# A two-block transformer kernel: the pool of operand slots moved to the upper end of the memory, above the weights' buffers

## The chip, the cores and the metric

The kernel runs on one core of a Trainium2 chip. The metric is the device time of one execution in microseconds (us). The core has TensorE (PE; its weight loads are listed as PEld), VectorE (DVE), ScalarE (ACT), GpSimd (POOL) and SyncE (SP), which here only issues DMAs. Operands lie in the on-chip memory SBUF, 128 partitions side by side; an address below is the byte at which a tile begins in each partition. Matmul results go to PSUM, a separate memory that the change does not touch.

## The reference

One sequence of 256 tokens with 1024 features passes through two blocks. The first has two layers: a gated linear recurrence (HGRN2) and a chunked band attention, each with a SwiGLU feed-forward network, all modulated by a vector c. The second mixes four kinds of attention (MoBA, NSA, differential, sliding window) and ends with a convolutional feed-forward network. All is float32. Nearly all of the arithmetic is in products of activations with weight matrices:

```
q, z_f, v, g = split(u @ w_in)                  # layer 0: HGRN2
h = h + g1 * mix;   u = modulate(rms_norm(h))
h = h + g2 * ((silu(gate) * up) @ w_out)        # gate, up = split(u @ w_in)
k, v = split(u @ w_kv);  q = u @ w_q            # layer 1: band attention
mix = concat(moba, nsa, diff, swa) @ w_out      # second block
x = x + rms_norm(conv_ffn(rms_norm(x)))
```

## The kernel before

Activations are kept transposed, features on the partitions and 256 tokens along each row. To reach float32 precision with fast matmuls, each operand is split into two float32r parts, hi and lo, and each product is three matmuls (`mm3`, L257 to L260): hi with hi, hi with lo, lo with hi. In `lin_A` (L262), `out_proj` (L302) and the feed-forward network's `down_T` the weights are loaded into the array and an activation of 256 columns is streamed; in `lin_B` (L280), `lin_Bt` and `down_B` an activation is loaded and the weights are streamed, in 512, 256 or 268 columns.

Weights arrive in units of up to 1088 float32 values per partition. `emit_dma` (L181) loads a unit into one of seven `w_raw` buffers through SP's queue, `emit_conv` (L188) makes `w_hi` on ACT (L193) and `w_lo` on DVE (L195), four buffers each. `pump` (L201) issues loads and conversions ahead of use, and `run` (L224) goes through a list of steps whose order is written out by hand. The instructions' order is therefore fixed when the program is built.

Memory is divided into pools (L144 to L147). `cst` holds constants. `big` holds eight operand slots `s0` to `s7` of 8,192 bytes, taken with `slot(i)` (L152): the residual stream `h` (s0), the hi and lo parts of the normed activations (s1 and s2, later also s3 to s7), the hidden activations (s5, s7), queries, keys and values. The inputs x are loaded into s5 and s6 (L389, L394, L396). `wts` holds the weights' buffers, `wk` small work tiles (`sq`, `nt`, `sig`, `rstd`, ...). Pools of the phases (`open_phase`, L161) hold tiles such as `att`, `lk`, `lq`, `pt` and the partial sums `ga`; they are opened and closed one after the other. A pool goes on top of the last one at the lower end of the memory, or, with `side="right"`, below the last one at the upper end. Before, only `wts` lies at the upper end. Line L350 takes 288 bytes without use (`gap`) among the constants, after which the slots begin at 30,720, a multiple of 2,048.

Of the kernel before, what the change touches and what calls it, by code (L numbers as in the profile page):

```python
# [131 lines left out]
def kernel(ctx: ExitStack, tc: tile.TileContext, x, c, mod_w, mod_b, norm_mix, norm_ffn,  # L132
# [9 lines left out]
    PE, DV, SC, GP, SY = nc.tensor, nc.vector, nc.scalar, nc.gpsimd, nc.sync  # L142

    cst = ctx.enter_context(tc.tile_pool(name="cst", bufs=1))  # L144
    big = ctx.enter_context(tc.tile_pool(name="big", bufs=1))
    wts = ctx.enter_context(tc.tile_pool(name="wts", bufs=1, side="right"))
    wk = ctx.enter_context(tc.tile_pool(name="wk", bufs=2))  # L147
    phase = {}
# [1749 lines left out]
```

## Time and profile before

| | |
|---|---|
| median of 3 runs | 1136.26 us (1135.9 to 1138.14) |
| profiled execution | 1137.38 us, of which the span from the first to the last instruction is 1135.6 us |
| mean granted TensorE clock | 0.996 |
| PE busy / weight loads | 97% / 89% |
| DVE, ACT, POOL busy | 67%, 50%, 12% |
| read from HBM | 239.33 MB, 212 GB/s over the span |

Busy time of PE counts overlapping matmuls; how far two starts are apart, in the timeline, tells the pace. In the rows, `pb_b<-s,w_hi` means that the matmul writes PSUM tile pb_b and reads a slot and w_hi; which of both is streamed is told by its place: the streamed operand stands first in these names where it is an activation (`s,w_hi`: the slot is streamed), and `w_hi,s` means that the weights are streamed and the slot is loaded. Buffer numbers are left out, so `s` is any of the eight slots.

### The profile page before, as it was taken

Reading aid. Unit: us, or ns where it says so; the run is one execution under the profiler, and the core shown is the slowest. Engines: PE = TensorE matmul, PEld = TensorE weight load, DVE = VectorE, ACT = ScalarE, POOL = GpSimd, SP = SyncE. Lnnn points to the kernel's source line nnn. Section 1 sums busy time; section 2 is a strip of 40 time slices with the busy share of each in tenths; the row PEclk is TensorE's granted clock in tenths of the full one; section 3 lists DMA queues with packets and bytes.
Section 4 is the critical chain, followed back from the end, with each engine's and each line's share of the span. In section 5 each row is a group of like instructions: output and inputs, shape, how many; then the busy total and the mean of one; then the engine's idle time right before and its main releaser. Section 6 shows DMA issues by size and latency. Waiting matters only on the chain.

```text
span 1135.6 us, 23604 instructions
## 1 busy us (share of the span) xinstructions
PE 1098.3 (97%) x9689; PEld 1014.6 (89%) x9689; DVE 763.1 (67%) x1237; ACT 572.9 (50%) x913; POOL 141.7 (12%) x201
## 2 busy tenths in 40 slices
PE   6899999999999999999999999999989999999997
PEld 4887888999999978788999999988879999999997
DVE  3577885777677598776555455677766766666676
ACT  2456464543444565655444344646655454454454
POOL 4044410000000001240000000024322110010010
PEclk9999999999999999999999999999998999999999
DMA  9976687898998597865765565873342655655651
GB/s 275 297 256 233 220 272 236 289 311 273 303 303 274 199 294 232 272 225 191 225 213 186 186 203 148 171 196 122 112 148 89 216 179 186 196 175 186 197 175 56
DMA packets 176124, 241.92 MB, mean 213 GB/s; under 512 B 18712, under 2 KB 142160, under 8 KB 176016
## 3 DMA queue, kind: packets, MB, share of 16 engines
q1 hardware_dynamic: 174928, 239.54, 66.8%
q8 instruction: 76, 1.25, 0.4%
q0 software_dynamic: 912, 0.81, 0.4%
q14 instruction: 32, 0.26, 0.1%
q10 hardware_dynamic: 176, 0.07, 0.0%
HBM read 239.33 MB, written 1.05 MB: 212 GB/s over the span
## 4 chain that ended last, share of the span: by engine, by line
PE 84%; DVE 5%; ACT 4%; DMA 3%; POOL 2%; issue 1%; SPq 0%; DVEq 0%; ACTq 0%; POOLq 0%
PE pb_b L258 15%; PE pb_b L260 15%; PE pb_b L259 14%; PE pb_acc L258 11%; PE pb_acc L260 10%; PE pb_acc L259 10%; DMA w_raw<-in_a_w_in_dram 2%; ACT w_hi L193 2%; DVE w_lo L195 2%; PE pb_b L463 1%; POOL dp L860 1%; PE pb_gv L524 1%; PE pb_b L1222 1%; DVE nt L573 1%; DMA w_raw<-in_mod_w_dram 1%
## 5 line engine op out<-in xcount | busy, mean ns | idle before, releaser
L195 DVE TENSOR_TENSOR w_lo<-w_raw,w_hi 128x1024 fp32r<-128x1024 f32 (+1 forms) x335 | 408.4, 1243 | 165.4 <-ACT w_hi L193 164.8
L258 PE MATMUL pb_b<-s,w_hi 128*128 128x256 f32 x1488 | 420.3, 282 | 5.3 <-ACT s L1756 2.9
L260 PE MATMUL pb_b<-s,w_lo 128*128 128x256 f32 x1488 | 417.4, 281 | 1.6 <-DVE w_lo L195 1.5
L259 PE MATMUL pb_b<-s,w_hi 128*128 128x256 f32 x1488 | 417.8, 281 | 0.3
L193 ACT CAST w_hi<-w_raw 128x1024 fp32r<-128x1024 f32 (+1 forms) x336 | 342.2, 1044 | 88.7 <-DMA w_raw<-in_a_w_in_dram 23.5
L258 PEld LDWEIGHTS pb_b<-s,w_hi 128*128 128x128 f32 x1488 | 281.0, 189 | 12.8 <-issue 4.0
L260 PEld LDWEIGHTS pb_b<-s,w_lo 128*128 128x128 f32 x1488 | 280.9, 189 | 2.5 <-DVE w_lo L195 2.4
L259 PEld LDWEIGHTS pb_b<-s,w_hi 128*128 128x128 f32 x1488 | 281.0, 189 | 1.9 <-DVE s L585 0.7
L258 PE MATMUL pb_acc<-s,w_hi 128*128 128x256 f32 x720 | 205.2, 285 | 1.8 <-ACT w_hi L193 1.7
L260 PE MATMUL pb_acc<-s,w_lo 128*128 128x256 f32 x720 | 201.5, 280 | 2.6 <-DVE w_lo L195 2.6
L259 PE MATMUL pb_acc<-s,w_hi 128*128 128x256 f32 x720 | 201.0, 279 | 0.1
L258 PEld LDWEIGHTS pb_acc<-s,w_hi 128*128 128x128 f32 x720 | 135.3, 188 | 9.2 <-issue 5.0
L260 PEld LDWEIGHTS pb_acc<-s,w_lo 128*128 128x128 f32 x720 | 135.3, 188 | 3.4 <-DVE w_lo L195 3.4
L259 PEld LDWEIGHTS pb_acc<-s,w_hi 128*128 128x128 f32 x720 | 135.4, 188 | 0.5 <-DVE s L585 0.3
L1215 POOL TENSOR_SCALAR att<-att,sm 128x128 f32<-128x128 f32 (+1 forms) x72 | 46.0, 657 | 617.4 <-DVE sm L1208 338.5
L1069 ACT CAST s<-sig 128x512 fp32r<-128x512 f32 x38 | 23.6, 621 | 117.6 <-DVE sig L1079 117.6
L258 PE MATMUL pb_acc<-w_hi,s 128*128 128x512 f32 x192 | 77.5, 404 | 1.4 <-ACT s L579 1.0
L259 PE MATMUL pb_acc<-w_lo,s 128*128 128x512 f32 x192 | 76.0, 396 | 0.8 <-DVE w_lo L195 0.8
L260 PE MATMUL pb_acc<-w_hi,s 128*128 128x512 f32 x192 | 76.1, 396 | 0.0
L1782 ACT ACTIVATE sig<-att,vb_t,vc_t 128x256 f32<-128x256 f32 x32 | 17.5, 594 | 75.4 <-DVE att L1777 75.4
L1792 POOL TENSOR_TENSOR sig<-sig,rstd 128x512 f32<-128x512 f32 x16 | 22.7, 1422 | 238.6 <-ACT sig L1790 238.6
L1075 ACT ACTIVATE sig<-pb_b 128x512 f32<-128x512 f32 x22 | 13.2, 598 | 75.1 <-PE pb_b L260 75.1
(367 smaller groups left out, 1166.6 us busy)
## 6 DMA issues: line engine op xcount, KB each, us to landing
w_raw<-in_mod_w_dram SPq DMA_DIRECT2D x96, 512.0 KB, 5.2
w_raw<-in_ffn_w_in_dram SPq DMA_DIRECT2D x88, 512.0 KB, 5.3
w_raw<-in_ffn_w_out_dram SPq DMA_DIRECT2D x44, 512.0 KB, 4.8
w_raw<-in_a_w_in_dram SPq DMA_DIRECT2D x32, 512.0 KB, 6.1
w_raw<-in_ffn_w_gate_dram SPq DMA_DIRECT2D x32, 512.0 KB, 3.7
w_raw<-in_ffn_w_up_dram SPq DMA_DIRECT2D x32, 512.0 KB, 5.4
w_raw<-in_ffn_w_down_dram SPq DMA_DIRECT2D x32, 512.0 KB, 3.5
w_raw<-in_kv_mod_w_dram SPq DMA_DIRECT2D x16, 512.0 KB, 5.6
```

What stands on the lines that cost most here:

```text
L193: SC.copy(hi, raw)
L195: DV.tensor_sub(lo, raw, hi.bitcast(F32))
L258: PE.matmul(o, lhsT=whi, rhs=xhi, start=start, stop=False, skip_group_check=True)
L259: PE.matmul(o, lhsT=whi, rhs=xlo, start=False, stop=False, skip_group_check=True)
L260: PE.matmul(o, lhsT=wlo, rhs=xhi, start=False, stop=stop, skip_group_check=True)
L463: PE.matmul(st[:, 0:256], lhsT=mean_d, rhs=sq[:, 256 * m:256 * m + 256], start=j == 0 and m == 0, stop=j == n - 1 and m == 1)
L524: PE.matmul(g[32 * j:32 * j + 32, 0:256], lhsT=by, rhs=r, start=start, stop=stop, tile_position=(0, 32 * j))
L1069: SC.copy(hi, hid)
L1075: SC.activation(sg, g, AF.Silu)
L1215: GP.tensor_scalar(t[:, i, cs], t[:, i, cs], r[:, 2 * b + i:2 * b + i + 1], 1.0, op0=OP.mult, op1=OP.mult)
L1782: SC.activation(zm, am, AF.Identity, bias=vcol("conv_b")[:, f:f + 1], scale=vc_t[:, 64 + f:65 + f])
L1792: GP.tensor_mul(zp, zp, rs_pair())
```

## The change

The pool `big` is given `side="right"`. As it is opened before `wts`, it takes the upper end, and the weights' buffers come directly below it. The work tiles and the phases' pools move down into the room that the slots leave.

```diff
     cst = ctx.enter_context(tc.tile_pool(name="cst", bufs=1))
-    big = ctx.enter_context(tc.tile_pool(name="big", bufs=1))
+    big = ctx.enter_context(tc.tile_pool(name="big", bufs=1, side="right"))
     wts = ctx.enter_context(tc.tile_pool(name="wts", bufs=1, side="right"))
     wk = ctx.enter_context(tc.tile_pool(name="wk", bufs=2))
```

On all five engines the instructions, their order and the semaphores that they wait for are the same in both programs. What differs are the addresses in the built programs:

| tiles | begin before | begin after | moved by | address past a multiple of 64, before and after |
|---|---|---|---|---|
| constants (`early`, `crep`, `late`, ...) | 16,512 to 25,440 | the same | 0 | unchanged |
| slots s5, s6, s0, s3, s4, s7, s1, s2 | 30,720 and on, each 8,192 | 163,808 and on, each 8,192 | +133,088 | 0, then 32 |
| `sq` (3 buffers) | 96,256 and on | 30,720 and on | -65,536 | 0, then 0 |
| other `wk` tiles and the phases' tiles | up to 163,998 | up to 98,462 | -65,536 | unchanged; `att`, `lk`, `lq`, `pt`: 32 |
| `w_raw` (7), `w_hi` (4), `w_lo` (4) | 164,064 to 229,344 | 98,528 to 163,808 | -65,536 | 32, then 32 |

## Rows read from the trace of the kernel before

**Rows 1.** The page: span, and busy time by engine.
```profile
span 1135.6 us, 23604 instructions
PE 1098.3 (97%) x9689; PEld 1014.6 (89%) x9689; DVE 763.1 (67%) x1237; ACT 572.9 (50%) x913; POOL 141.7 (12%) x201
```

**Rows 2.** The page: chain that ended last, by engine and by line.
```profile
PE 84%; DVE 5%; ACT 4%; DMA 3%; POOL 2%; issue 1%; SPq 0%; DVEq 0%; ACTq 0%; POOLq 0%
PE pb_b L258 15%; PE pb_b L260 15%; PE pb_b L259 14%; PE pb_acc L258 11%; PE pb_acc L260 10%; PE pb_acc L259 10%; DMA w_raw<-in_a_w_in_dram 2%; ACT w_hi L193 2%; DVE w_lo L195 2%; PE pb_b L463 1%; POOL dp L860 1%; PE pb_gv L524 1%; PE pb_b L1222 1%; DVE nt L573 1%; DMA w_raw<-in_mod_w_dram 1%
```

**Rows 3.** Groups by line and shape, TensorE: count, busy us, mean ns, idle before.
```profile
L259 PE MATMUL pb_b<-s,w_hi 128*128 128x256 f32 x1488 | 417.8, 281 | 0.3
L259 PEld LDWEIGHTS pb_b<-s,w_hi 128*128 128x128 f32 x1488 | 281.0, 189 | 1.9 <-DVE s L585 0.7 <-DVE s L1758 0.2
L259 PE MATMUL pb_acc<-s,w_hi 128*128 128x256 f32 x720 | 201.0, 279 | 0.1
L259 PE MATMUL pb_acc<-w_lo,s 128*128 128x512 f32 x192 | 76.0, 396 | 0.8 <-DVE w_lo L195 0.8
L259 PEld LDWEIGHTS pb_acc<-w_lo,s 128*128 128x128 f32 x192 | 36.1, 188 | 8.4 <-DVE w_lo L195 1.1
L259 PE MATMUL pb_b<-w_lo,s 128*128 128x256 f32 x32 | 9.0, 281 | 0.0
```

**Rows 4.** Timeline of TensorE, slots streamed: start us, us, engine, line, operation.
```profile
239.75 0.28 PE L260 MATMUL pb_b<-s,w_lo 128*128 128x256 f32 x1
...
242.11 0.28 PE L259 MATMUL pb_acc<-s,w_hi 128*128 128x256 f32 x1
...
289.73 0.28 PE L258 MATMUL pb_b<-s,w_hi 128*128 128x256 f32 x1
...
291.72 0.28 PE L260 MATMUL pb_b<-s,w_lo 128*128 128x256 f32 x1
```

**Rows 5.** Timeline of TensorE, weights streamed, in 512 and in 256 columns.
```profile
483.80 0.39 PE L259 MATMUL pb_acc<-w_lo,s 128*128 128x512 f32 x1
...
486.81 0.40 PE L260 MATMUL pb_acc<-w_hi,s 128*128 128x512 f32 x1
...
807.88 0.28 PE L260 MATMUL pb_b<-w_hi,s 128*128 128x256 f32 x1
...
810.36 0.28 PE L260 MATMUL pb_b<-w_hi,s 128*128 128x256 f32 x1
```

**Rows 6.** Timeline of TensorE, line L463, `sq` or `att` streamed.
```profile
715.91 1.02 PE L463 MATMUL pb_b<-sq,early 128*128 128x256 f32 x4
716.77 1.03 PE L463 MATMUL pb_b<-att,early 128*128 128x256 f32 x4
717.63 1.03 PE L463 MATMUL pb_b<-sq,early 128*128 128x256 f32 x4
```

**Rows 7.** Groups by line and shape, ACT and DVE (last row: ns min/median/max).
```profile
L1198 ACT ACTIVATE att<-att,mx 128x256 f32<-128x256 f32 x40 | 19.8, 496 | 0.0
L518 DVE SCALAR_TENSOR_TENSOR lk<-w_raw,ca,lk 128x512 f32<-128x512 f32 x28 | 20.9, 746 | 0.0
L1317 ACT ACTIVATE s<-s,cols 128x256 fp32r<-128x256 f32 x8 | 3.6, 496 | 2.2 <-DVE s L1314 2.2
L1820 DVE SCALAR_TENSOR_TENSOR ot<-ot,ms,s x4: 743/748/751, 1128.4 to 1131.9; 128x512 f32<-128x512 f32 x4
```

**Rows 8.** Groups by line and shape on POOL, and who waited for it.
```profile
L877 POOL TENSOR_TENSOR s<-s,dp 128x256 f32<-128x256 f32 x20 | 17.7, 898 | 17.1 <-PE pb_b L900 9.6 <-PE pb_b L919 7.4
L1755 POOL TENSOR_TENSOR s<-s,nt 128x256 f32<-128x256 f32 x8 | 6.7, 875 | 17.3 <-DVE nt L1753 17.3
L877 POOL TENSOR_TENSOR s<-s,s 128x256 f32<-128x256 f32 x4 | 4.5, 1140 | 3.6 <-ACT a L908 3.6
PE pb_b L900 <- POOL s L877: 1.3, 1, 1.3
```

**Rows 9.** DMA issues: count, KB each, median us to landing.
```profile
w_raw<-in_mod_w_dram SPq DMA_DIRECT2D x96, 512.0 KB, 5.2
s<-in_x_dram SPq DMA_DIRECT2D x2, 512.0 KB, 4.1
```

## The prediction

> **What bounds the kernel now.** I read the page from the top: span and busy shares, then the chain of waits, then the groups by line and shape, then the timeline of single matmuls. TensorE is busy 97% of the span [rows 1], and 84% of the chain that ended last is TensorE; the three matmul lines L258 to L260 alone hold 15 + 14 + 15 + 11 + 10 + 10 = 75% of it, or 852 us of 1135.6 [rows 2]. The reader should see that nothing else comes near: DVE has 5%, ACT 4%, DMA 3% and POOL 2% of the chain.
>
> So the question is what one matmul costs and whether that depends on where its operands lie. The groups give the counts: 1488 matmuls on each of the three lines into pb_b and 720 into pb_acc stream a slot (`s`) against weights, 3 x (1488 + 720) = 6624 in all, with 128x256 operands; 192 per line stream the weights in 512 columns, and 32 per line in 256 [rows 3]. The busy time of one (281 ns) overlaps with its neighbours, so the pace has to be read from start to start: 289.73 to 291.72 us holds 17 steps, 0.117 us each; 239.75 to 242.11 holds 20 steps, 0.118 us each [rows 4]. 6624 x 0.117 us = 775 us is the part of the span that streams slots.
>
> **The change part by part.** It adds no instruction and removes none; each engine issues the same operations in the same order behind the same waits in both programs. Every effect must come from addresses. There are two moves.
>
> First, everything but the slots and the constants goes down by 65,536 bytes. That is the same shift for the weights' buffers, the work tiles and the tiles of the phases, and 65,536 is a multiple of every power of two up to itself, so their alignment and their distances to each other stay. I cost this at nothing. What it changes is their distance to the slots, which I take with the second move.
>
> Second, the slots go up by 133,088 bytes, which is 65 x 2,048 less 32. Before, each slot begins at a multiple of 2,048; after, each begins 32 bytes past a multiple of 64, as the weights' buffers do in both versions. So kernel before already runs both kinds of operand, and its rows can be set side by side.
>
> - *TensorE, streaming operand.* A slot streamed in 256 columns has a busy time of 281 ns; the weights streamed in 256 columns, which begin 32 bytes past a multiple of 64, have 281 ns too [rows 3]. The cleanest pair is line L463, where the same constant is loaded and the streamed tile is once `sq` (at a multiple of 2,048) and once `att` (32 past a multiple of 64): four `sq` take from 715.91 to 716.77, four `att` from 716.77 to 717.63, 0.86 us each [rows 6]. These are full fp32 matmuls at about half the pace, so they could hide a stall that float32r matmuls would show. The paces of the float32r matmuls bound it: 512 columns of weights take (486.81 - 483.80) / 13 = 0.2315 us, or 0.1158 per 256, and 256 columns of weights take (810.36 - 807.88) / 21 = 0.1181 [rows 5]. Against 0.117 that is -1.2 ns and +1.1 ns for each of 6624 matmuls: -7.9 to +7.3 us. I take 0, because the two ends have opposite signs for the same kind of address, and because slots at unchanged addresses run at 0.117 in one stretch and 0.118 in another [rows 4], so a nanosecond comes and goes without any move.
> - *TensorE, loaded operand.* Loading weights takes 189 ns, loading a slot 188 ns [rows 3]. 0.
> - *ACT and DVE.* The same operation costs the same at both kinds of address: on ACT 496 ns on `att` and 496 ns on slots (128x256), on DVE 746 ns on `lk` and `w_raw` and 748 ns on `ot` with a slot (128x512) [rows 7]. 0, and TensorE covers both engines in most of the span.
> - *POOL.* No row has a two-input POOL operation on misplaced operands alone. The 20 products of line L877 average 898 ns and four others of the same line 1140 ns [rows 8]; if all 20 went to the dearer row it would be 20 x 0.242 = 4.8 us, if they went down to the 875 ns of L1755, -0.5 us. TensorE waited only 1.3 us for L877 in this execution [rows 8], so little of either end reaches the span. I take 0.
> - *Loads into slots.* Only the two loads of x land in slots (median 4.1 us each); loads of the same 512 KB into the misplaced `w_raw` land in 5.2 us, with more queued ahead of them [rows 9]. If x took that, it would be up to 1.1 us late at the very start; below nothing there is no reason to go, since 4.1 is already the shorter. I take 0. The Trainium skill (DMA: Bandwidth & Descriptors, How a descriptor splits into AXI transactions) speaks against the change here: a descriptor that does not begin at a multiple of 256 B starts its first transaction at the boundary below and pays for bytes that it does not use. By it a 4 KB row of x would need 8 more beats on 128, about 6%; as an estimate from that and the two landings that is 0.25 us on each load, and the sum would be 1136.8 instead of 1136.3. No run here shows it yet.
>
> Sum: 0 + 0. The profiled execution took 1137.38 us, 1.8 us of it outside its span of 1135.6 [rows 1]; it lies 1.1 us above the median of the three timed runs, 1136.26, so the forecast on the median's scale is 1136.3 us. The fixed work in it is the same, whatever the layout.
>
> **The rivals.**
>
> *Slower: the stream from a misplaced slot stalls.* Place: the 6624 matmuls that stream a slot. For it: the 256-column stream of weights paces 0.1181 us against 0.117 [rows 4, 5], the only row with a float32r matmul, the same width and the other kind of address. Against it: the 512-column stream, misplaced alike, is the cheapest per column; L463 shows no difference; the slots themselves reach 0.118 at times. Price: 6624 x 1.1 ns = 7.3 us if all of it is on the path. Nearly all matmuls of the three lines pace 775 + 576 x 0.2315 + 96 x 0.118 = 920 us, and the chain holds 852 of them, 93%: 6.8 us, or 1143.1 us. It decides from 2.3 us / (6624 x 0.93) = 0.37 ns a matmul upward, about a third of the difference that this row suggests, so a partial effect gives 1139 to 1143.
>
> *Faster: the placement next to the weights, or the new alignment, gives slots the pace of the 512-column rows.* For it: 0.1158 per 256 columns [rows 5]. Against it: that gain goes as well with the half as many instructions per column, and the 256-column stream of weights doesn't have it. Price: 6624 x 1.2 ns x 0.93 = 7.4 us, or 1128.9.
>
> *Neighbours get in each other's way.* Slots now lie directly above the buffers that DMA, ACT and DVE fill. If reads and writes of close addresses collided, a matmul that streams the weights' own buffers would already show it, and its 512-column pace is the best there is [rows 5]. If it cost the difference of the two slot paces, 1 ns, it would give 6624 x 1 ns x 0.93 = 6.2 us, 1142.4.
>
> *It does not do what it says.* The slots could have stayed where they were; the addresses of the built program exclude it. A change of waits through reused memory is excluded too, since slots share no memory with other tiles in either version.
>
> **How the numbers follow.** No effect: 0.68, with its own range of 1134.0 to 1138.6, 2.3 us to either side (the three runs of before lie between 1135.9 and 1138.14). The stalled stream, full or in part: 0.18; neighbours: 0.06. The fast pace, full or in part: 0.08. A measurement of this kernel can tell about 0.2%, 2.3 us, from no change, and that gives faster 0.08, same 0.68, slower 0.24. The range goes from 1133.6 to 1143.2: it takes in the whole of no effect and the slower cases to their price, and leaves out most of the faster case and what lies beyond the slower ones.
>
> **What would show it.** Right: start to start of L258 to L260 on slots at 0.117 to 0.118 us in the same stretches, weight loads at 188 ns, TensorE's waits as before, x landing within 0.3 us of before. Wrong: a pace on slots of 0.118 to 0.119 or more in stretches that had 0.117 (stalled stream), above all if 512-column matmuls keep 0.2315; or longer ACT, DVE and POOL operations on slots alone, which I have put at nothing.

## The result, and the profile after

The changed kernel is slower: 1151.32 us against 1136.55 us, ratio 1.0123 (95% interval 1.0099 to 1.0146). The forecast was 1136.3 us with a range from 1133.6 to 1143.2. The profiled execution took 1151.56 us.

The first lines of the page, to be read beside [rows 1] and [rows 2], and the groups of TensorE that answer to [rows 3]:

```profile
span 1149.8 us, 23604 instructions
PE 1113.6 (97%) x9689; PEld 1032.9 (90%) x9689; DVE 763.6 (66%) x1237; ACT 572.1 (50%) x913; POOL 140.0 (12%) x201
PE 85%; DVE 5%; ACT 4%; DMA 3%; issue 2%; POOL 1%; SPq 0%; DVEq 0%; ACTq 0%; POOLq 0%
```

```profile
L259 PE MATMUL pb_b<-s,w_hi 128*128 128x256 f32 x1488 | 422.9, 284 | 0.3
...
L259 PE MATMUL pb_acc<-s,w_hi 128*128 128x256 f32 x720 | 204.2, 284 | 0.0
...
L259 PE MATMUL pb_acc<-w_lo,s 128*128 128x512 f32 x192 | 75.1, 391 | 0.8 <-DVE w_lo L195 0.8
...
L259 PE MATMUL pb_b<-w_lo,s 128*128 128x256 f32 x32 | 9.0, 282 | 0.0
```

```profile
L259 PEld LDWEIGHTS pb_b<-s,w_hi 128*128 128x128 f32 x1488 | 285.8, 192 | 1.8 <-DVE s L585 0.7 <-DVE s L1758 0.3
...
L259 PEld LDWEIGHTS pb_acc<-w_lo,s 128*128 128x128 f32 x192 | 36.1, 188 | 7.6 <-DVE w_lo L195 1.1
```

The span grew by 14.2 us, TensorE's busy time by 15.3 us, DVE's by 0.5 us, ACT's and POOL's not at all; the shares of these three in the chain did not grow. So the loss is TensorE's. A matmul that streams a slot went from 281 (279 into pb_acc) to 284 ns, its weight load from 189 to 192 ns. One that streams the weights in 512 columns went the other way, from 396 to 391 ns, and its load, now of a slot at the other kind of address, stayed at 188.

Busy times overlap, so the pace is read from start to start. The first two rows are of the kernel before, the next four of the kernel after: 60 steps in the same part of the program (L258 to L260, no wait in them), and then 21 steps in 512 columns.

```profile
684.07 0.28 PE L258 MATMUL pb_b<-s,w_hi 128*128 128x256 f32 x1
...
691.07 0.28 PE L258 MATMUL pb_acc<-s,w_hi 128*128 128x256 f32 x1
```

```profile
690.21 0.28 PE L258 MATMUL pb_b<-s,w_hi 128*128 128x256 f32 x1
...
697.40 0.28 PE L258 MATMUL pb_acc<-s,w_hi 128*128 128x256 f32 x1
```

```profile
491.30 0.39 PE L260 MATMUL pb_acc<-w_hi,s 128*128 128x512 f32 x1
...
496.07 0.40 PE L260 MATMUL pb_acc<-w_hi,s 128*128 128x512 f32 x1
```

7.00 us / 60 = 116.7 ns before, 7.19 / 60 = 119.8 ns after; three matmuls (one `mm3`) take 350 ns and then 360. In 512 columns it is 4.77 / 21 = 227.1 ns, where [rows 5] gave 231.5.

The same can be taken over a whole trace: from every start of L258 to the next start of L258, where L258, L259 and L260 follow without a wait (some 2020 such triples stream a slot, some 150 stream weights in 512 columns). All paces below are these means. Slots: 117.0 ns before, 119.9 after. 512 columns: 234.1 before, 229.5 after. In 512 columns some 15 triples take 770 to 820 ns where the others take 700 or 680, and how many of these are counted moves the mean by about 1 ns. The sum that follows: 6624 x 2.9 = 19.2 us lost, 576 x 4.6 = 2.6 us gained, and of the 16.6 us the 93% that the prediction put on the path are 15.4; measured 14.2 on the spans and 14.8 on the medians.

What the prediction also put at nothing stayed there. Line L463 takes 0.86 us for four `sq` as in [rows 6], ACT and DVE cost what they cost in [rows 7], POOL what it cost in [rows 8]:

```profile
724.40 1.02 PE L463 MATMUL pb_b<-sq,early 128*128 128x256 f32 x4
725.26 1.03 PE L463 MATMUL pb_b<-att,early 128*128 128x256 f32 x4
```

```profile
L1198 ACT ACTIVATE att<-att,mx 128x256 f32<-128x256 f32 x40 | 19.8, 496 | 0.0
...
L877 POOL TENSOR_TENSOR s<-s,dp 128x256 f32<-128x256 f32 x20 | 17.5, 891 | 17.0 <-PE pb_b L900 9.5 <-PE pb_b L919 7.5
...
L1317 ACT ACTIVATE s<-s,cols 128x256 fp32r<-128x256 f32 x8 | 3.6, 495 | 2.4 <-DVE s L1314 2.4
```

```profile
s<-in_x_dram SPq DMA_DIRECT2D x2, 512.0 KB, 4.7
```

The loads of x landed after 4.7 us instead of 4.1 [rows 9]. The new address need not be the reason: with the slots where the kernel before has them, a later run (slots 0, weights 0) showed 4.9, and with slots 32 bytes lower another (slots 32, weights 32) showed 4.2. The spread between runs hides the 0.25 us that the prediction estimated from the Trainium skill (DMA: Bandwidth & Descriptors, How a descriptor splits into AXI transactions); no run here shows it.

### The profile page after: what moved, and what is told of

Same layout as the page of the kernel before. It is cut to its first block, busy times and chain, and to the rows that moved or that the text cites. A ratio compares the mean times of both kernels' runs of the same rounds, so it can differ in the third digit from the quotient of the medians.

```text
span 1149.8 us, 23604 instructions
## 1 busy us (share of the span) xinstructions
PE 1113.6 (97%) x9689; PEld 1032.9 (90%) x9689; DVE 763.6 (66%) x1237; ACT 572.1 (50%) x913; POOL 140.0 (12%) x201
## 4 chain that ended last, share of the span: by engine, by line
PE 85%; DVE 5%; ACT 4%; DMA 3%; issue 2%; POOL 1%; SPq 0%; DVEq 0%; ACTq 0%; POOLq 0%
PE pb_b L258 15%; PE pb_b L260 15%; PE pb_b L259 14%; PE pb_acc L258 11%; PE pb_acc L260 10%; PE pb_acc L259 10%; DVE w_lo L195 2%; DMA w_raw<-in_a_w_in_dram 1%; ACT w_hi L193 1%; PE pb_b L463 1%; PE pb_b L1222 1%; DMA w_raw<-in_kv_w_dram 1%; PE pb_gv L524 1%; DMA w_raw<-in_mod_w_dram 1%; POOL dp L860 1%
## 5 line engine op out<-in xcount | busy, mean ns | idle before, releaser
L258 PE MATMUL pb_b<-s,w_hi 128*128 128x256 f32 x1488 | 424.8, 285 | 5.1 <-ACT s L1756 2.9
L260 PE MATMUL pb_b<-s,w_lo 128*128 128x256 f32 x1488 | 421.9, 284 | 1.5 <-DVE w_lo L195 1.4
L259 PE MATMUL pb_b<-s,w_hi 128*128 128x256 f32 x1488 | 422.9, 284 | 0.3
L258 PEld LDWEIGHTS pb_b<-s,w_hi 128*128 128x128 f32 x1488 | 285.7, 192 | 12.5 <-issue 4.4
L260 PEld LDWEIGHTS pb_b<-s,w_lo 128*128 128x128 f32 x1488 | 285.9, 192 | 2.4 <-DVE w_lo L195 2.3
L259 PEld LDWEIGHTS pb_b<-s,w_hi 128*128 128x128 f32 x1488 | 285.8, 192 | 1.8 <-DVE s L585 0.7
L258 PE MATMUL pb_acc<-s,w_hi 128*128 128x256 f32 x720 | 208.3, 289 | 1.8 <-ACT w_hi L193 1.8
L260 PE MATMUL pb_acc<-s,w_lo 128*128 128x256 f32 x720 | 204.5, 284 | 1.5 <-DVE w_lo L195 1.5
L259 PE MATMUL pb_acc<-s,w_hi 128*128 128x256 f32 x720 | 204.2, 284 | 0.0
L258 PEld LDWEIGHTS pb_acc<-s,w_hi 128*128 128x128 f32 x720 | 138.4, 192 | 9.1 <-issue 4.8
L260 PEld LDWEIGHTS pb_acc<-s,w_lo 128*128 128x128 f32 x720 | 138.6, 192 | 2.1 <-DVE w_lo L195 2.1
L259 PEld LDWEIGHTS pb_acc<-s,w_hi 128*128 128x128 f32 x720 | 138.5, 192 | 0.2
L258 PE MATMUL pb_acc<-w_hi,s 128*128 128x512 f32 x192 | 76.7, 400 | 1.5 <-ACT s L579 1.0
L259 PE MATMUL pb_acc<-w_lo,s 128*128 128x512 f32 x192 | 75.1, 391 | 0.8 <-DVE w_lo L195 0.8
L260 PE MATMUL pb_acc<-w_hi,s 128*128 128x512 f32 x192 | 75.1, 391 | 0.0
```

The costliest lines, as they stand in the source:

```text
L258: PE.matmul(o, lhsT=whi, rhs=xhi, start=start, stop=False, skip_group_check=True)
L259: PE.matmul(o, lhsT=whi, rhs=xlo, start=False, stop=False, skip_group_check=True)
L260: PE.matmul(o, lhsT=wlo, rhs=xhi, start=False, stop=stop, skip_group_check=True)
```

## The experiments

All kernels below issue the same instructions in the same order; only addresses differ. "Slots 32" means that the slots begin 32 bytes past a multiple of 64, "weights 32" the same of `w_hi` and `w_lo`. Ratios are to the kernel before, with their 95% intervals.

### First four: is it the place, or 32 bytes?

Three theories. A: the distance between slots and weights counts, taken modulo 64 (equal: 360 ns per three; 32 apart: 350). B: the slots' own start counts. C: the place of the pools counts (the upper end, or lying beside the weights' buffers).

The changed layout, with the slots 32 bytes lower and so on a multiple of 64 again:

```diff
 # on the changed kernel
-        lo = wts.tile([P, UNIT], F32R, name="w_lo", ...)[:, :n]
+        lo = wts.tile([P, UNIT], F32R, name="w_lo", ...)[:, :n]; state["pad"] = state.get("pad") or wts.tile([P, 8], F32, name="pad_w", bufs=1)
-            ubox[tag] = (hi, lo)
+            ubox[tag] = (hi, lo); state["pad_s"] = state.get("pad_s") or big.tile([P, 8], F32, name="pad_s", bufs=1)
```

> The changed kernel's layout (slots above the weights' buffers), with 32 bytes of padding behind the slots and behind the weights' buffers: slots begin at multiples of 64 again, the weights' buffers stay 32 past one. Theory A (what counts is where the slot begins relative to the weights, in the address bits below 64: 32 apart 0.117 us, equal 0.120 us a streamed 256-column matmul): 1136 us, pace 0.117. Theory B (what counts is the slot's own start: at a multiple of 64 0.117, past one 0.120): 1136 us as well. Theory C (the place: upper end, next to the weights' buffers): stays at 1151 us, pace 0.120.

Measured: 1136.63 us, ratio 1.0003 (0.9989 to 1.0017), slots at 116.9 ns. Sixty steps of it:

```profile
684.02 0.28 PE L258 MATMUL pb_b<-s,w_hi 128*128 128x256 f32 x1
...
691.02 0.28 PE L258 MATMUL pb_acc<-s,w_hi 128*128 128x256 f32 x1
```

The whole loss is gone with 32 bytes, at the upper end and beside the weights. C is out.

The layout of before, the slots alone 32 bytes lower:

```diff
-    wk = ctx.enter_context(tc.tile_pool(name="wk", bufs=2))
+    wk = ctx.enter_context(tc.tile_pool(name="wk", bufs=2)); wk.tile([P, 8], F32, name="pad_wk", bufs=1)
-    cst.tile([P, 72], F32, name="gap")
+    cst.tile([P, 64], F32, name="gap")
```

> The layout of before, with the slots alone 32 bytes lower (32 past a multiple of 64, as the weights' buffers); work tiles and weights unmoved. Theories A and B: 1151 us, pace 0.120 on slots, and 0.227 for 512 columns as in the changed kernel. Theory C (place): 1136 us, pace 0.117.

Measured: 1154.44 us, ratio 1.0158 (1.0132 to 1.0183), slots at 119.9 ns, 512 columns at 229.1. The loss is made without moving a pool:

```profile
690.31 0.28 PE L258 MATMUL pb_b<-s,w_hi 128*128 128x256 f32 x1
...
697.50 0.28 PE L258 MATMUL pb_acc<-s,w_hi 128*128 128x256 f32 x1
```

Then the weights' buffers 32 bytes lower, alone (slots 0, weights 0), and together with the slots (slots 32, weights 0); the edits are `pad_w` above, and `pad_w` with the smaller gap.

> The layout of before, with the weights' buffers alone 32 bytes lower, so that slots and weights both begin at multiples of 64. Theory A (relative): as the changed kernel, 1151 us, pace 0.120 on slots. Theory B (the slot's own start): pace 0.117 and 1136 us. Theory C: 1136 us.

> The layout of before, with slots 32 past a multiple of 64 and weights' buffers at multiples of 64: the offsets of before, exchanged. Theory A (relative): pace 0.117 and 1136 us. Theory B (the slot's own start): 0.120 and 1151 us. Theory C: 1136 us.

Measured: 1137.56 us, ratio 1.0004 (0.9989 to 1.0020), and 1137.01 us, 0.9994 (0.9981 to 1.0007). The first contradicts A (equal starts modulo 64, and no loss), the second contradicts B (slots 32, and no loss).

### Next four: a pair of misplaced operands?

What was left was theory D: a matmul pays when both its operands are 32 past a multiple of 64. One edit tests its parts, because a buffer of 1088 values has room to write the parts further in; here only `w_lo` (32 bytes further, on a multiple of 64), in the kernel with slots 32 and weights 32:

```diff
-        lo = wts.tile([P, UNIT], F32R, name="w_lo", tag="w_lo", bufs=WT_BUFS)[:, :n]
+        lo = wts.tile([P, UNIT], F32R, name="w_lo", tag="w_lo", bufs=WT_BUFS)[:, 8:8 + n]
```

> Slots begin 32 bytes past a multiple of 64 as in the run that alone had its slots lowered (1154.4 us), w_hi too, but w_lo begins on a multiple of 64. Of every three matmuls two load w_hi and one loads w_lo, so one of three now has no pair of misplaced operands. Theory D (each matmul pays for its own pair: +3 ns only where its streamed and its loaded operand both begin past a multiple of 64): two thirds of the loss stay, three matmuls take 2 x 120 + 117 = 357 ns, about 1148.5 us. Theory E (the stream of matmuls falls into one common rhythm, which any break of the pattern undoes): three matmuls take 350 to 353 ns as before, about 1137 us. Rival F (one misplaced pair in the three is enough for the slow rhythm): 360 ns, about 1154 us.

> The mirror image: slots 32 past a multiple of 64, w_hi on a multiple, w_lo 32 past it. One matmul of three has both operands misplaced. Theory D (each matmul pays for its own pair): one third of the loss stays, 117 + 117 + 120 = 354 ns, about 1142.5 us. Theory E (common rhythm, undone by any break): 350 to 353 ns, about 1137 us. Rival F (one pair is enough): 360 ns, about 1154 us.

Measured: `w_lo` moved, 1146.21 us, ratio 1.0063 (1.0043 to 1.0084), 355 ns per three; `w_hi` moved instead, 1142.53 us, 1.0036 (1.0022 to 1.0050), 353.3 ns per three. The loss comes in parts, more with two bad loads in the three than with one; E (a common rhythm, undone by any break: 1137 us for both) and F (one pair is enough: 1154 us) lie outside both intervals. D comes nearest without hitting: it forecast 357 and 354 ns, 1148.5 and 1142.5 us, the first above its interval.

Then `w_hi` and `w_lo` 16 bytes further (`[:, 4:4 + n]`), with slots 32 and with slots 0:

> Slots 32 past a multiple of 64, w_hi and w_lo 48 past one instead of 32 (w_raw stays). Theory D as 'any start past a multiple of 64 counts': both operands are misplaced, 120 ns per 256 columns, about 1154 us. Theory G, that the two starts must stand at the same place within 64 bytes on top of being misplaced: 117 ns, about 1137 us. If a start on a multiple of 32 is what matters and 48 is worse than 32, more than 120 ns and over 1156 us.

> Slots on a multiple of 64 as in the kernel before, w_hi and w_lo 48 past one instead of 32. Theories D and G both: only one operand is misplaced, 117 ns per 256 columns, about 1136.5 us. If the distance to the next multiple of 64 set a price by itself, another pace; a rhythm at 113.3 ns throughout, as parts of the run with both operands on multiples of 64 showed it, would give about 1136.5 - 6624 x 3.7 ns x 0.93 = 1114 us.

Measured: 1144.46 us, ratio 1.0058 (1.0041 to 1.0075), 355 ns per three; and 1148.95 us, 1.0090 (1.0067 to 1.0113), 352 ns in some stretches and 360 in others. Neither D (1154 and 1136.5 us) nor G (1137 and 1136.5 us) forecasts them. The second is a loss with slots on a multiple of 64.

### D put to use, and its fall

By D the changed kernel could be mended: loaded weights on a multiple of 64, streamed ones (512 columns, which had become faster) left as they were. The same offsets in the layout of before as a control.

```diff
 # on the changed kernel; Unit keeps off; unit_A and unit_row take it, 8 where nothing is given
-        hi = wts.tile([P, UNIT], F32R, name="w_hi", tag="w_hi", bufs=WT_BUFS)[:, :n]
+        hi = wts.tile([P, UNIT], F32R, name="w_hi", tag="w_hi", bufs=WT_BUFS)[:, u.off:u.off + n]
 # (and w_lo the same way)
-        ... [unit_A(w, 256 * i, c0, 2, 512)] ...
+        ... [unit_A(w, 256 * i, c0, 2, 512, 0)] ...
-        ... unit_row(w_out, 256 * (rounds - 1) + P * i) ...
+        ... unit_row(w_out, 256 * (rounds - 1) + P * i, 8 * (down.__name__ != "down_B")) ...
```

> The changed kernel's layout (slots at the upper end, 32 bytes past a multiple of 64) with one thing added: w_hi and w_lo are written 8 values (32 bytes) into their buffers, so that they begin on a multiple of 64, except the units whose weights are streamed in 512 columns (lin_B and down_B, 576 matmuls), which stay 32 past it like the slots that they meet. Theory D (a price for each matmul whose streamed and loaded operand are both 32 past a multiple of 64, +3 ns on 256 columns, and a gain on 512): the 256-column matmuls run at 350 ns per three as in the run with slots 32 and weights 0, the 512-column ones at 229.5 ns instead of 234.1, so 576 x 4.6 ns x 0.93 = 2.5 us below before: about 1134 us, ratio 0.998. If the gain on 512 columns belonged to the upper end or to something else: 1136.5 us. If the pool's place has a part in the loss: over 1140 us.

> The same offsets in the layout of the kernel before: slots at the lower end, 32 past a multiple of 64, weights' buffers on a multiple of 64, and only the weights that are streamed in 512 columns written 32 bytes further in. Theory D: as the run beside it, about 1134 us, ratio 0.998, with 350 ns per three 256-column matmuls and 229.5 ns per 512-column one. Rival: the 512-column pace hangs on w_raw or on the place of the pools, then 1136.5 us and 234 ns.

Measured: the mended changed kernel 1145.54 us, ratio 1.0086 (1.0067 to 1.0104), slots at 118.4 ns; the control 1136.66 us, 1.0003 (0.9986 to 1.0019), slots at 117.0 ns, 512 columns at 229.3 as forecast. (The 2.5 us that this should bring are not shown: 0.998 lies just outside the interval, although the slots' pace is that of before; why is open.) Two kernels that are alike to D differ by 9 us. The first came out where the rival "the pool's place has a part in the loss" had it; the run with slots 64 lower, below, decides on that. Rows of the first, two stretches of sixty steps:

```profile
321.19 0.28 PE L258 MATMUL pb_b<-s,w_hi 128*128 128x256 f32 x1
...
328.39 0.28 PE L258 MATMUL pb_b<-s,w_hi 128*128 128x256 f32 x1
...
684.09 0.28 PE L258 MATMUL pb_b<-s,w_hi 128*128 128x256 f32 x1
...
691.18 0.28 PE L258 MATMUL pb_b<-s,w_hi 128*128 128x256 f32 x1
```

7.20 / 60 = 120.0 and 7.09 / 60 = 118.2 ns: 360 and 355 per three, never 350.

What does differ is the distance, if it is not cut at 64 bytes. Where a slot is streamed it is the loaded operand's start less the streamed one's, that is `w_hi`'s start less a slot's start, modulo 256: 224 before, 0 in the changed kernel, 224 in the two harmless runs with one pool shifted (slots 0 and weights 32 at the upper end; slots 32 and weights 0 at the lower), 192 with slots 0 and weights 0, 32 in the mended kernel. Slots are 8,192 bytes apart and cut at 1,024, buffers 4,352 (17 x 256) and cut at 512, so one number serves for all matmuls of a kernel that stream a slot against weights. This is theory H: the distance alone counts, modulo 256. It is theory A with a longer period, and it was made from these ten runs, so it needed runs that could refute it.

### One number, moved in steps

The slots alone go lower by 64, 96, 128, 160 and 192 bytes in the layout of before; the constants behind the gap go with them. For 96:

```diff
-    wk = ctx.enter_context(tc.tile_pool(name="wk", bufs=2))
+    wk = ctx.enter_context(tc.tile_pool(name="wk", bufs=2)); wk.tile([P, 24], F32, name="pad_wk", bufs=1)
-    cst.tile([P, 72], F32, name="gap")
+    cst.tile([P, 48], F32, name="gap")
```

> The layout of the kernel before, the slots begin 64 bytes lower than there (the constants behind the unused bytes with them), the weights' buffers stay. Slots begin on a multiple of 64 again, w_hi and w_lo 32 past one; w_hi's start less a slot's start is 32 above a multiple of 256 (before: 224, in the slow run with slots 32 lower: 0). Theory D (a price where both operands are 32 past a multiple of 64): only one is, so 350 ns per three matmuls, 1136.5 us. Theory H (only the distance between the two starts counts, modulo 256; 0 gives 360 ns, 32 gives 355 and in stretches 360 as in the mended changed kernel): 355 to 357 ns, about 1136.5 + 2208 x 6 ns x 0.93 = 1149 us at most, 1145 us by that kernel.

> Slots 96 bytes lower than before, 32 past a multiple of 64 like the weights' buffers; distance 64 modulo 256. Theory D: 360 ns per three matmuls and 1154 us as with 32 lower. Theory H: a distance not yet measured, so anything between 340 and 360, but no reason for 360 throughout; by its neighbour 32 about 350 to 355 ns, 1137 to 1145 us.

Measured: 64 lower, 1146.30 us, ratio 1.0076 (1.0048 to 1.0103); 96 lower, 1128.12 us, 0.9910 (0.9882 to 0.9939). D forecast no loss for the first and the full loss for the second; both came out the other way. The first also has the time of the mended changed kernel (1145.54 us), which stands at the same distance with the pools the other way round, so the place of the pools is not needed for that loss. The first, at distance 32, sixty steps, and the second, at distance 64, two stretches of sixty:

```profile
684.10 0.28 PE L258 MATMUL pb_b<-s,w_hi 128*128 128x256 f32 x1
...
691.20 0.28 PE L258 MATMUL pb_b<-s,w_hi 128*128 128x256 f32 x1
```

```profile
592.18 0.28 PE L258 MATMUL pb_b<-s,w_hi 128*128 128x256 f32 x1
...
598.98 0.28 PE L258 MATMUL pb_acc<-s,w_hi 128*128 128x256 f32 x1
...
684.25 0.28 PE L258 MATMUL pb_acc<-s,w_hi 128*128 128x256 f32 x1
...
691.31 0.28 PE L258 MATMUL pb_b<-s,w_hi 128*128 128x256 f32 x1
```

7.10 / 60 = 118.3 ns at distance 32. At 64 it is 6.80 / 60 = 113.3 in one stretch and 7.06 / 60 = 117.7 in the other, with no slower one.

> Slots 128 bytes lower than before, on a multiple of 64; distance 96 modulo 256. Theory D: 350 ns, 1136.5 us. Theory H: not yet measured; if the pace falls steadily from distance 0 to the far side (0: 360, 32: 355, and 224: 350, 192: 340 to 353), 340 to 350 ns, 1113 to 1136 us. If what counted were the distance modulo 128, it would equal before's 224: 350 ns, 1136.5 us.

> Slots 160 bytes lower than before, 32 past a multiple of 64 like the weights' buffers; distance 128 modulo 256. Theory D: 360 ns, 1154 us. Theory H with modulus 256: the far side, 340 ns if the pace falls steadily with the distance, 1136.5 - 2208 x 10 ns x 0.93 = 1116 us. Theory H with modulus 128: equal to distance 0, 360 ns and 1154 us, the same as D; the run at 64 lower tells those two apart.

> Slots 192 bytes lower than in the kernel before, distance 160 modulo 256. Theory H with modulus 128: as distance 32, 355 ns per three matmuls and 1145 to 1146 us. With modulus 256: a distance of its own, between the neighbours 128 (356 to 360 ns) and 192 (340 and 353 ns), so 345 to 357 ns, 1127 to 1147 us. Theory D: 350 ns, 1136.5 us.

Measured: 1144.75 us, ratio 1.0063 (1.0038 to 1.0088); 1147.29 us, 1.0094 (1.0062 to 1.0127); 1154.36 us, 1.0153 (1.0118 to 1.0188). A period of 128 is out: 160 is not like 32 (360 ns per three against 355, and the intervals of the ratios lie apart), nor 96 like 224 (352 and 356 against 350 and 353). The pace does not fall steadily with the distance, as I had thought it might.

The test of "alone": the changed kernel with `w_hi` and `w_lo` 64 bytes further in, so that both operands are still 32 past a multiple of 64, but 64 apart.

```diff
 # on the changed kernel
-        hi = wts.tile([P, UNIT], F32R, name="w_hi", tag="w_hi", bufs=WT_BUFS)[:, :n]
-        lo = wts.tile([P, UNIT], F32R, name="w_lo", tag="w_lo", bufs=WT_BUFS)[:, :n]
+        hi = wts.tile([P, UNIT], F32R, name="w_hi", tag="w_hi", bufs=WT_BUFS)[:, 16:16 + n]
+        lo = wts.tile([P, UNIT], F32R, name="w_lo", tag="w_lo", bufs=WT_BUFS)[:, 16:16 + n]
```

> The changed kernel with one addition: w_hi and w_lo are written 16 values (64 bytes) into their buffers. Slots and weights both stay 32 past a multiple of 64; only the distance between them goes from 0 to 64 modulo 256. Theory H (the distance alone counts): the paces of the run with slots 96 lower, 340 and 353.3 ns per three matmuls by stretches, mean 115.4 ns, and its time of 1128 us, ratio 0.991. Theory D (each start modulo 64): as the changed kernel, 360 ns, 1151 us. If the place of the pools has a share: between the two.

Measured: 1128.19 us, ratio 0.9919 (0.9895 to 0.9944), with slots at 115.9 ns. Its span, TensorE's busy time and two stretches of sixty steps:

```profile
span 1126.8 us, 23604 instructions
PE 1087.9 (97%) x9689; PEld 1006.8 (89%) x9689; DVE 762.2 (68%) x1237; ACT 572.7 (51%) x913; POOL 140.8 (12%) x201
```

```profile
684.23 0.28 PE L258 MATMUL pb_acc<-s,w_hi 128*128 128x256 f32 x1
...
691.30 0.28 PE L258 MATMUL pb_b<-s,w_hi 128*128 128x256 f32 x1
...
1018.26 0.28 PE L258 MATMUL pb_b<-s,w_hi 128*128 128x256 f32 x1
...
1025.06 0.28 PE L258 MATMUL pb_b<-s,w_hi 128*128 128x256 f32 x1
```

The first stretch runs at 7.07 / 60 = 117.8 ns, slower than the same part of the kernel before (116.7); the gain lies in stretches like the second, 6.80 / 60 = 113.3 ns.

The pools lie as the change lays them, and the time is 23 us below the changed kernel and 8.6 us below the one before: the same time as with slots 96 lower, where the pools lie the other way round. The sum holds here too: 6624 x 1.1 ns and 576 x 3.7 ns (512 columns at 230.4) are 9.4 us, 93% of it 8.8.

The two neighbours, 48 in the changed kernel (`[:, 12:12 + n]`) and 80 (slots 96 lower, `[:, 4:4 + n]`), to see whether 64 is the best place:

> The changed kernel with w_hi and w_lo 12 values (48 bytes) into their buffers: distance 48 modulo 256. Theory H: a distance not yet measured, between 32 (355 ns per three matmuls in all stretches, or 360 in some) and 64 (340 or 353 ns); 345 to 355 ns, 1128 to 1146 us. If the weights' start at an odd multiple of 16 costs by itself, as at distances 16 and 240: 352 to 360 ns, 1142 to 1150 us.

> The run with slots 96 lower (1128.1 us), with w_hi and w_lo 4 values (16 bytes) into their buffers: distance 80 modulo 256. Theory H: between 64 (340 or 353 ns per three matmuls) and 96 (352 or 356 ns): 340 to 356 ns, 1115 to 1146 us; a time under 1127 us would be a better place than 64, over 1129 us a worse one.

Measured: 1151.41 us, ratio 1.0130 (1.0099 to 1.0162), and 1146.93 us, 1.0088 (1.0058 to 1.0119). 64 is the best of twelve distances, and 16 bytes to either side of it cost over 18 us. Whether that cost comes from the distance is not separated: 16, 48, 80 and 240 were all made by letting the weights begin at an odd multiple of 16, all four are losses, and the rival that such a start costs by itself was not tested alone (at 48 it had forecast 1142 to 1150 us, nearer to the 1151.41 than theory H with 1128 to 1146).

All distances together (pace: slots streamed, mean per matmul; per three: the paces that hold through a stretch):

| distance mod 256 | kernel | ratio | pace, ns | per three, ns | 512 columns, ns |
|---|---|---|---|---|---|
| 0 | changed; slots 32 lower | 1.0123; 1.0158 | 119.9; 119.9 | 360 | 229.5; 229.1 |
| 16 | slots 32, weights 48 | 1.0058 | 118.3 | 355 | 232.5 |
| 32 | 64 lower; changed, mended by D | 1.0076; 1.0086 | 118.3; 118.4 | 355; 355 and 360 | 234.2; (at 0) 230.8 |
| 48 | changed, weights 48 bytes in | 1.0130 | 119.4 | 353 and 370 | 234.6 |
| 64 | 96 lower; changed, weights 64 bytes in | 0.9910; 0.9919 | 115.4; 115.9 | 340 and 353 | 230.4; 230.4 |
| 80 | 96 lower, weights 16 bytes in | 1.0088 | 118.7 | 356 | 232.6 |
| 96 | 128 lower | 1.0063 | 118.1 | 352 and 356 | 233.9 |
| 128 | 160 lower | 1.0094 | 119.0 | 356 and 360 | 233.9 |
| 160 | 192 lower | 1.0153 | 120.0 | 360 | 235.1 |
| 192 | slots 0, weights 0 | 1.0004 | 116.9 | 340 and 353 | 234.2 |
| 224 | before; slots 0 at the upper end; slots 32, weights 0; control | 1; 1.0003; 0.9994; 1.0003 | 117.0; 116.9; 116.8; 117.0 | 350 and 353 | 234.1; 234.2; 234.0; (at 0) 229.3 |
| 240 | slots 0, weights 48 | 1.0090 | 118.3 | 352 and 360 | 235.7 |

"(At 0)" marks the two kernels whose streamed weights stand at distance 0 to the slots that they meet. Distances 0, 32, 64 and 224 were run in two to four different layouts, and each time the intervals of the ratios overlap. At 32, 64 and 224 the layouts also differ in where each operand begins modulo 256; at 0 both kernels have it at 224, so there the distance was not varied apart from the start. The two runs that mix 0 and 32 (`w_lo` or `w_hi` moved alone) are not in the table: 355 and 353.3 ns per three are no more than either distance alone, the second less than both (355 and 360), so prices of single matmuls do not add up to the three's. A period of 256 fits all; a longer one is not needed, since the buffers stand alternately at 0 and 256 modulo 512 and the pace doesn't alternate.

Every trace holds a second test, which needed no run of its own: the 96 matmuls that stream weights in 256 columns and load a slot. With the roles exchanged, the loaded operand's start less the streamed one's is the negative: 32 before, 64 in the run with slots 0 and weights 0, 224 in the run with slots 64 lower. If this difference counts, they must have the paces that slots have at those distances:

```profile
813.59 0.28 PE L260 MATMUL pb_b<-w_hi,s 128*128 128x256 f32 x1
...
815.97 0.28 PE L260 MATMUL pb_b<-w_hi,s 128*128 128x256 f32 x1
```

```profile
822.08 0.28 PE L260 MATMUL pb_b<-w_hi,s 128*128 128x256 f32 x1
...
824.53 0.29 PE L260 MATMUL pb_b<-w_hi,s 128*128 128x256 f32 x1
```

The first pair of rows is of slots 0, weights 0: 2.38 / 21 = 113.3 ns, 340 per three, as slots have it at 64. The second is of slots 64 lower: 2.45 / 21 = 116.7, 350 per three, as at 224. Before, [rows 5] give 118.1, as slots at 32 (118.3). At all distances that are multiples of 32 the mean of such triples in a trace (24, without the first of each group) lies within 1.2 ns of a pace that the table has at the negative distance, or between its two paces. Where the weights begin at an odd multiple of 16, two can be compared: 240 agrees (353.2 ns, between 352 and 360), 16 does not (351.5 against 355).

A collision of TensorE's reads with what ACT and DVE write into `w_hi` and `w_lo` meanwhile is a rival that the trace of the changed kernel excludes: 270 of its triples on slots ran while ACT, DVE and POOL did nothing, and 268 of these took 360 ns. `w_raw`, into which the DMAs write, lies unmoved in the run that ended the loss (weights 64 bytes in).

## Why the prediction was wrong

*What bounds the kernel, the counts, the share on the path:* right. 6624 matmuls at a pace, 93% of it on the path, turned the paces into the measured difference to within 3 us in the changed kernel and in all 18 runs, losses and gains alike.

*That only addresses change, and that ACT, DVE, POOL, the loads of x and the waits don't matter:* right, by the rows above. In the estimate from the Trainium skill (DMA: Bandwidth & Descriptors, How a descriptor splits into AXI transactions) a 4 KB row that begins 224 bytes past a multiple of 256, as after the change, needs 7 beats more, not 8.

*"TensorE, streaming operand", valued at 0 between -1.2 and +1.1 ns:* this step failed. It measured +2.9 ns. The prediction asked of each operand whether it begins on a multiple of 64, and said that the kernel "before already runs both kinds of operand". It had promised to take the distance between slots and weights with the second move, and then never did. In before the float32r matmuls that stream a slot against weights all stand at one distance, 224 modulo 256, those with the roles exchanged at 32, and the change turns both into 0: slots up by 133,088 and weights down by 65,536 make 198,624, which is 775 x 256 + 224. No row of before shows distance 0, so no row could price it. The rows that were set side by side differed in something else: those of 512 columns and of L463 in the number of columns, the type or the loaded tile. L463 in full fp32 did stay at 0.86 us, and it said nothing on float32r, as the prediction itself feared; its `sq` and `att` moved by 65,536, a multiple of 256, so its distance to the constant that is loaded had not changed either. The bounds were too narrow for that reason: the lower came from another number of columns, the upper from distance 32. Its 1.1 ns were a real price, of the distance and not of the address, and were valued at 0. Nor was the nanosecond between 0.117 and 0.118 on slots one that "comes and goes": these are the two fixed paces of distance 224, 350 and 353 ns per three, either of which holds through a stretch.

*"Loaded operand", 0:* also missed, 189 to 192 ns. No second cost is added here, since the paces alone give 15.4 us and 14.2 to 14.8 were measured. Which of the two, the stream or the load, holds up the other is not shown.

*The rival "stream from a misplaced slot stalls":* right in the place, the sign and the matmuls, wrong in its cause and so in its price (1143.1 us). A slot at the same misplaced address costs nothing at distance 224 (1137.01 us) and runs faster than before at distance 64 (1128.19 us). Its mark, that the 512-column matmuls would keep their pace, was wrong as well: they got faster.

*The rival "faster":* refuted for this change, since the slots' pace went from 117.0 to 119.9 ns; a faster place does exist, at distance 64 and not by alignment.

*The rival "neighbours":* refuted by the run at the upper end with slots 0, 1136.63 us.

The cause is shown down to the addresses: the distance between the streamed and the loaded operand, for distances that are multiples of 32. Why a distance of 0 or 160 is bad and 64 is good, that is what in the memory or in TensorE's reading collides, is not shown by any run here. Nor is it shown why the mended kernel, at distance 32, has stretches at 360 ns beside 355, when the kernel with slots 64 lower has 355 alone.

## What to carry to other kernels

When a change moves pools and TensorE is the bound, write down the distance between the streamed and the loaded operand of the commonest matmul, here modulo 256, before and after; if it changes, rows that stand at other distances bound nothing, however many of them show each operand's own alignment. A scan is worth its runs: steps of 32 bytes found 0.8 to 0.9% here, and the worst and the best place are 2.3% apart (1154 and 1128 us). Choose a theory's test where it and its rival differ in sign: D came near in some runs and missed others, and one step of 96 bytes, a loss by D and a gain when measured, ended it.

## What the runs showed of the hardware

Float32r matmuls of 256 columns run in a few fixed paces: 340, 350, 352, 353.3, 355, 356, 360 and 370 ns per three, as means over twenty `mm3`, were seen to hold for tens of microseconds. The granted clock in such stretches was 1.00 of full speed (592 to 599 us in the run with slots 96 lower, 690.2 to 697.4 after), the level of 2.4 GHz; by it 340 and 360 ns are 816 and 864 cycles, or 272 and 288 for each matmul of 256 columns.

Where a distance has two paces, the one that runs is kept as long as the stream is not broken. Each of the 20 traces has 44 or 45 unbroken streams of 14 to 270 `mm3` on slots, and behind the first few `mm3` all but one in each of the two kernels at distance 64 keep one pace to the end. Behind a break it can be the other: in the run with slots 0 and weights 0, 21 steps at (873.89 - 871.51) / 21 = 113.3 ns come before a wait for `w_lo`, and 21 at (877.45 - 874.98) / 21 = 117.6 ns behind it, with the same operands' distance:

```profile
871.51 0.28 PE L258 MATMUL pb_b<-s,w_hi 128*128 128x256 f32 x1
...
873.89 0.28 PE L258 MATMUL pb_b<-s,w_hi 128*128 128x256 f32 x1
...
874.76 0.38 PE L260 MATMUL pb_b<-s,w_lo 128*128 128x256 f32 x1 [0.47 <-DVE w_lo L195]
874.98 0.28 PE L258 MATMUL pb_b<-s,w_hi 128*128 128x256 f32 x1
...
877.45 0.28 PE L258 MATMUL pb_b<-s,w_hi 128*128 128x256 f32 x1
```

So two kernels at one distance can differ by what their long streams fell into (115.4 and 115.9 ns at 64). At distance 64, 340 ns throughout would, as an estimate from these paces, bring 6624 x (115.4 - 113.3) ns x 0.93 = 13 us on top of the best kernel; what sets the pace behind a wait, no run here tells.
